# A22 × T4 of each two pairs of the MLP by seven half-size inner products, in a kernel of eight cores

## The chip, the cores and the metric

The kernel runs on the eight cores of one Trainium2 chip (two dies of four cores). Each core takes 1024 tokens and all weights; the cores exchange nothing. The metric is the device time of the slowest core in microseconds (us), over several executions.

Some executions fall into a slower state in which one or both dies run at a lower granted TensorE clock (in the profile of before die 1 had 0.967 and its cores took 1120.7 us, die 0 had 0.993 and 1091.8 us, medians of the cores). Every run is marked *fast* or *slow* for that, and only fast runs are compared here. A ratio is the mean time of one kernel's fast runs over the mean of the other's fast runs of the same rounds on the same chip. That is not quite the ratio of the medians that are quoted beside it.

## The reference, cut to what matters

The function is a decoder block: a token mixer (gating heads and pooling heads), an output projection, then a squared-ReLU MLP.

```python
D_MODEL, D_FF = 2048, 8192          # x is (2, 4096, 2048): 1024 tokens for each of eight cores
def reference(x, ...):
    ...                              # mixer and output projection, about the first 310 us
    # rmsnorm(x, g_ffn), h @ w_up, relu squared, @ w_down, residual; then the final rmsnorm
    ...
```

The MLP is done in four blocks of 2048 hidden channels. A block has an *up* part (h2T times w_up) and a *down* part (the activations `mlp` times w_down). Each part is eight *pairs*; a pair is two tiles of 128 output channels. The eight parts run from about 310 to 1040 us of the span.

## The kernel before

On each core TensorE does the matrix products, VectorE and ScalarE the sums, copies and activations, and DMA transfers are requested from queues, here mostly from the Pool queue (109.85 of the 144.48 MB in the profile of before). The kernel has TensorE add up each product in a bank of the tile `ps`, which is called a PSUM bank here. A program is written as a list of operations; a scheduler on the host, which is part of the kernel, fixes each engine's order before the launch. TensorE keeps the order in which the program writes its products. VectorE and ScalarE get an order from estimated times, the Pool queue keeps the order of the program. On the chip each engine then goes through its list in one order: all eight cores show the same sequence on VectorE (1254 instructions), ScalarE (959) and Pool (273), though their waits differ.

**A pair.** Contraction 2048 and 1024 tokens are split in halves. With A11, A12 (first tile), A21, A22 (second tile) and B11 … B22 the four blocks are made by seven products instead of eight (Strassen–Winograd). Each product is a group of eight matmuls with 512 columns. The letters below are the kernel's own:

| letter | product | letter | product |
|---|---|---|---|
| n | A11 × B11 of the *next* pair | 5 | S1 × T1 |
| 2 | A12 × B21 | 4 | A22 × T4 |
| 6 | S2 × T2 | 3 | S4 × B22 |
| 7 | S3 × T3 | | |

S1 … S4 are sums of weight blocks that VectorE makes anew for each pair. T1 … T4 are sums of activation blocks, made once for each part. n, 6, 7 and 4 add up in one PSUM bank; after n, 6 and 7 ScalarE copies the partial sum out, and the next of them may not start before that copy.

**Two pairs.** For 26 couples of pairs (an even and an odd one: 15 couples in up parts, 11 in down parts) product 2 is not made by two groups of 8 × 512. A12 of both pairs times B21 is again split in halves and made by seven products, each four matmuls of 256 columns: `q w y r` and two of `e` in the even pair, one more `e` in the odd pair.

```python
NORMAL, LAST, FIRST = "6275n43", "625s7n4", "5627n43"
NORMAL_A, NORMAL_B, LAST_B, FIRST_A = "q65w7enyr43", "657en43", "6e5s7n4", "56qe7wnyr43"

def q_sums(i):                                  # left sums of two pairs, on VectorE
    a, b = A(i, 0, 1), A(i + 1, 0, 1)           # A12 of pair i and of pair i+1
    ...
    qs[1] = ... Sq[:, 0] = b[:, 0::2, :] + b[:, 1::2, :]
    qs[2] = dve_sub(Sq[:, 1], Sq[:, 0], a[:, 0::2, :], ...)
    qs[4] = dve_sub(Sq[:, 2], a[:, 1::2, :], Sq[:, 1], ...)

def inner(c, i, R, st, b21):                    # q, w and y add up in one bank, with a copy after each
    if c == "q":
        ... pe(mms4(b, 0, A(i, 0, 1)[:, 0::2, :], I.b11, True), ...)
        q_op["s", 0] = P.add("act", ... sq[:, 0, :] <- ps[:, b, 0:HQ] ...)
    elif c == "w":
        ... pe(mms4(b, 0, Sq[:, 1], I.t2, False), ...)          # needs the copy of q
        q_op["s", 1] = P.add("act", ... sq[:, 1, :] <- ps ...)
    elif c == "y":
        ... pe(mms4(b, 0, A3(i), I.t3, False), ...)             # needs the copy of w
    ...
```

Note that the sums for `w` in the even pair i read a tile of pair i+1.

**Weight tiles.** Each pair has two tiles of 128 × 2048. They arrive in a ring of six slots, so the tiles of pair i+3 take the slots of pair i. Their requests are issued from the Pool queue when the next pair begins. In the down parts that queue also carries the accumulating stores of finished results.

```python
def load_tiles(upto=NTILE):                     # asks for tiles as long as the next slot's user is done
    while nxt[0] <= min(upto, NTILE - 1):
        ...
        elif u is not None and done[u] is None:
            break
        ...
        tile_ld[n] = P.dma("pool", ... TL(n) <- wt_d[n - NSTART] ...)

# in pair(): both slots count as done after the pair's last product
if c in "43s":
    tile_done[n0] = tile_done[n1] = st[4 if c == "4" else 3]
# in the loops over pairs: load_tiles() is called first, then pair(...)
# in StageEnd (down parts): the store, in the same Pool queue
stg_last[s] = xo_last[m, h] = P.dma("pool", ... xo_d[m] <- stg, accum_op=ALU.add ...)
```

## Time and profile before

| | us |
|---|---|
| median of the first three runs | 1090.83 (1089.46 to 1154.0, of which 1154.0 is slow) |
| fast runs | 1089.46, 1089.61, 1090.83 |

This is the view of all cores: span and mean granted clock of a core, then the median of each die.

```profile
core 0: 1092.2 us, clock 0.993
...
die 0 (median of its cores): 1091.8 us, clock 0.993
die 1 (median of its cores): 1120.7 us, clock 0.967
```

Die 0 was hardly disturbed, so core 0 is read. First the page of core 0: busy us of each engine, its share of the span, and the number of instructions; then the chain of waits, the work that ended last followed back to its releasers, as shares of the span.

```profile
PE 1070.8 (98%) x5952; PEld 548.9 (50%) x5952; DVE 684.2 (63%) x1254; ACT 473.3 (43%) x959; POOL 170.9 (16%) x273
...
PE 93%; DMA 3%; DVE 2%; POOL 1%; issue 1%; ACT 0%; DVEq 0%; ACTq 0%; POOLq 0%
```

TensorE (PE) is the bound: 98% busy and 93% of the chain. The 3% of DMA in the chain is the start of the kernel, not the MLP's tiles.

Next the timeline of TensorE on core 0 (start, duration, engine, line, operation, destination and sources, size, count), cut to the borders of two pairs in an up part. Rows of four 256-wide matmuls and of sixteen 512-wide ones let the durations be taken from start to start.

```profile
504.88 0.60 PE L537 MATMUL ps<-h2T,ring 128*128 128x256 bf16 x4
505.32 3.62 PE L537 MATMUL ps<-T,Sw 128*128 128x512 f16 x16
508.77 0.60 PE L537 MATMUL ps<-TH,Sq 128*128 128x256 f16 x4
...
517.86 3.62 PE L537 MATMUL ps<-T,Sw 128*128 128x512 f16 x16
...
528.66 0.60 PE L537 MATMUL ps<-h2T,ring 128*128 128x256 bf16 x4
```

The two pairs take 528.66 − 504.88 = 23.78 us: 12.98 for the even pair and 10.80 for the odd one. Sixteen 512-wide matmuls take 3.45 us, four 256-wide ones 0.44 us. No row carries a wait. Busy time alone would not prove that: the record of four small matmuls is 0.60 us long and the next row starts 0.44 us after it. So a record can reach 0.16 us into the next one, and a gap of less than 0.16 us does not show in the busy share here.

Last, a down part: the timeline of core 0 with all engines, cut to the store and the tile requests in the Pool queue, the first left sum that reads the tile on VectorE (DVE), and `w` on TensorE, which needs two such sums.

```profile
874.51 3.62 PE L537 MATMUL ps<-Q,Sw 128*128 128x512 f16 x16
...
876.13 0.88 POOL L1495 DMA_DIRECT2D xo<-stg  x1 [1.89 <-DVE stg L955]
...
876.70 1.44 POOL L610 DMA_DIRECT2D ring<-wt  x2
...
887.40 0.43 DVE L989 TENSOR_TENSOR Sq<-ring 128x512 f16<-128x512 bf16 x1 [0.54 <-DMA ring<-wt]
...
889.20 0.60 PE L537 MATMUL ps<-TH,Sq 128*128 128x256 f16 x4
```

The odd pair begins at 874.51.

### The profile page before, as it was taken

Reading aid. Unit: us, or ns where it says so; the run is one execution under the profiler, and the core shown is the slowest. Engines: PE = TensorE matmul, PEld = TensorE weight load, DVE = VectorE, ACT = ScalarE, POOL = GpSimd, SP = SyncE. Lnnn points to the kernel's source line nnn. Section 1 sums busy time; section 2 is a strip of 40 time slices with the busy share of each in tenths; the row PEclk is TensorE's granted clock in tenths of the full one; section 3 lists DMA queues with packets and bytes.
Section 4 is the critical chain, followed back from the end, with each engine's and each line's share of the span. In section 5 each row is a group of like instructions: output and inputs, shape, how many; then the busy total and the mean of one; then the engine's idle time right before and its main releaser. Section 6 shows DMA issues by size and latency. Waiting matters only on the chain.

```text
span 1122.8 us, 17577 instructions; the slowest of 8 cores (1091.3 to 1122.8 us)
## 1 busy us (share of the span) xinstructions
PE 1094.4 (97%) x5871; PEld 556.7 (50%) x5952; DVE 685.2 (61%) x1254; ACT 476.6 (42%) x959; POOL 170.4 (15%) x273
## 2 busy tenths in 40 slices
PE   5899999999999999999999999999999999999997
PEld 1354444444444444554454555544455544455577
DVE  1559547866687665555556555555665555556657
ACT  2421166545455552113555211355522135555574
POOL 4210024300000002221000222100022210001000
PEclk9999999999999999999999999999999999999999
DMA  9999504678768857999454799945579996469408
GB/s 213 266 169 166 94 1 80 139 197 173 139 136 161 184 98 98 133 130 139 79 92 77 101 132 133 140 75 90 80 98 134 138 167 102 80 131 202 76 6 297
DMA packets 51052, 144.48 MB, mean 129 GB/s; under 512 B 6482, under 2 KB 13650, under 8 KB 50580
## 3 DMA queue, kind: packets, MB, share of 16 engines
q0 software_dynamic: 33936, 109.85, 63.5%
q1 hardware_dynamic: 17028, 33.50, 9.5%
q8 instruction: 49, 0.80, 0.3%
q14 instruction: 39, 0.32, 0.1%
HBM read 204.14 MB, written 28.32 MB: 207 GB/s over the span
## 4 chain that ended last, share of the span: by engine, by line
PE 93%; DMA 2%; issue 2%; DVE 2%; POOL 1%; ACT 0%; DVEq 0%; ACTq 0%; POOLq 0%
PE ps L537 93%; DMA ring<-wt 2%; DVE xr_all L1615 1%; POOL ring L580 0%; DVE xh L1615 0%; POOL xst L571 0%; DVE xh L1363 0%; DVE xr_all L1363 0%; ACT sqB L1385 0%; ACT xr_all L1353 0%; DVEq L1650 0%; DVE xr_all L1392 0%; DVE xr_all L1382 0%; DVE xB L1615 0%; ACT sqr L1367 0%
## 5 line engine op out<-in xcount | busy, mean ns | idle before, releaser
L610 POOL DMA_DIRECT2D ring<-wt x158 | 92.9, 639 | 525.5 <-PE ps L537 519.4
L975 ACT ACTIVATE UC<-ps 128x512 f32<-128x512 f32 (+1 forms) x144 | 83.8, 582 | 206.5 <-PE ps L537 189.9
L537 PE MATMUL ps<-hT,ring 128*128 128x512 bf16 x501 | 118.6, 391 | 16.5 <-DMA ring<-w 14.5
L955 DVE TENSOR_TENSOR xr_all<-xr_all,ps 128x512 f32<-128x512 f32 (+1 forms) x102 | 67.2, 660 | 106.8 <-PE ps L537 106.7
L537 PE MATMUL ps<-Q,Sw 128*128 128x512 f16 x512 | 117.8, 380 | 0.0
L537 PE MATMUL ps<-T,Sw 128*128 128x512 f16 x512 | 117.6, 382 | 0.0
L537 PE MATMUL ps<-mlp,ring 128*128 128x192 bf16 (+4 forms) x755 | 100.4, 282 | 1.1
L537 PEld LDWEIGHTS ps<-hT,ring 128*128 128x128 bf16 x512 | 50.4, 100 | 80.5 <-issue 26.4
L537 PE MATMUL ps<-h2T,ring 128*128 128x512 bf16 (+1 forms) x361 | 85.5, 377 | 2.6
L955 DVE TENSOR_TENSOR rtmp<-UC,ps 128x512 f32<-128x512 f32 x64 | 43.9, 685 | 71.9 <-PE ps L537 56.9
L1432 ACT ACTIVATE rtmp<-rtmp 128x512 f32<-128x512 f32 x94 | 58.8, 629 | 67.2 <-DVE rtmp L955 67.2
L1435 ACT ACTIVATE mlp<-rtmp 128x512 bf16<-128x512 f32 x128 | 77.4, 625 | 5.8
L537 PE MATMUL ps<-h2T_t,wring 128*128 128x512 f16 (+1 forms) x316 | 79.7, 398 | 0.0
L537 PEld LDWEIGHTS ps<-Q,Sw 128*128 128x128 f16 x512 | 50.2, 98 | 58.7 <-issue 1.7
L537 PEld LDWEIGHTS ps<-T,Sw 128*128 128x128 f16 x512 | 50.3, 98 | 57.0 <-issue 2.9
L537 PEld LDWEIGHTS ps<-mlp,ring 128*128 128x128 bf16 x776 | 60.9, 99 | 33.8 <-issue 4.0
L1495 POOL DMA_DIRECT2D xo<-stg x48 | 42.4, 884 | 223.2 <-DVE stg L955 208.6
L972 ACT ACTIVATE ps<-ps 128x512 f32<-128x512 f32 (+1 forms) x72 | 41.0, 570 | 62.7 <-PE ps L537 61.6
L537 PE MATMUL ps<-T,ring 128*128 128x512 f16 x256 | 63.9, 395 | 0.0
L537 PEld LDWEIGHTS ps<-h2T,ring 128*128 128x128 bf16 x392 | 41.4, 106 | 41.6 <-issue 30.0
L537 PE MATMUL ps<-h2T,Sw 128*128 128x512 bf16 x252 | 60.8, 385 | 0.2
L537 PE MATMUL ps<-Q,ring 128*128 128x512 f16 x256 | 60.8, 381 | 0.0
(182 smaller groups left out, 1613.5 us busy)
## 6 DMA issues: line engine op xcount, KB each, us to landing
ring<-wt POOLq DMA_DIRECT2D x158, 512.0 KB, 9.0
xo<-stg POOLq DMA_DIRECT2D x48, 256.0 KB, 5.5
xr_all<-xr SPq DMA_DIRECT2D x10, 512.0 KB, 12.3
out<-xr_all SPq DMA_DIRECT2D x11, 384.0 KB, 3.7
xst<-xs POOLq DMA_DIRECT2D x8, 512.0 KB, 23.1
xo<-xr_all SPq DMA_DIRECT2D x8, 512.0 KB, 5.7
xr_all<-xo SPq DMA_DIRECT2D x8, 512.0 KB, 8.8
xst<-xs POOLq DMA_DIRECT2D x3, 1024.0 KB, 22.1
```

Source lines behind the costliest of these rows:

```text
L537: op = P.add("pe", lambda e, o=o, l=l, r=r, st=st, sp=sp: e.matmul(o, l, r, start=st, stop=sp, skip_group_check=True))
L610: tile_ld[n] = P.dma("pool", lambda e, n=n: e.dma_start(out=TL(n), in_=wt_d[n - NSTART].rearrange("p (k c) -> p k c", k=KC)), "t%d" % s, deps)
L955: return P.add("dve", lambda e: e.tensor_tensor(out=out, in0=x, in1=y, op=ALU.add), deps)
L972: st["cp", 0] = P.add("act", lambda e: e.activation(out=ps[:, b, 0:w], in_=ps[:, st["a"], 0:w], func=AF.Copy), [st[1], bank_last[b]])
L975: st["cp", u + 1] = P.add("act", lambda e: e.activation(out=UC[:, u, 0:w], in_=ps[:, st["a"], 0:w], func=AF.Copy), [st[which], uc_rd[u]])
L1432: a1 = P.add("act", lambda e: e.activation(out=t, in_=src, func=AF.Relu, scale=CA), [ready, free])
L1435: rt_rd[s] = done[h] = P.add("act", lambda e: e.activation(out=mlp[:, f, h * H:(h + 1) * H], in_=t, func=AF.Square), [a1] + deps)
L1495: stg_last[s] = xo_last[m, h] = P.dma("pool", lambda e: e.dma_start(out=xo_d[m][:, h * H:(h + 1) * H], in_=t, accum_op=ALU.add), "sg%d" % ...
L1615: o = P.add("dve", lambda e: e.tensor_tensor(out=y, in0=x, in1=r.to_broadcast(list(x.shape)), op=ALU.mult), r3[g])
```

## The change

The intent: do for product 4 (A22 × T4) what is done for product 2 already. Two groups of 8 × 512 per couple are replaced by seven products of 4 × 256, written with capital letters Q W Y R E. Their left sums, copies and right sums get buffers of their own, most of them in memory that only the last weight tiles used before; two right sums of the down parts and two of the left sums lie elsewhere, as the diff shows. The code for the small letters becomes a class that serves both.

```diff
+    TH4 = sb("TH4", [128, 3, 4, HQ], F16, LOW)
+    TA44 = sb("TA44", [128, 4, HQ], F16, LOW + 6144)
+    sq4 = sb("sq4", [128, 4, HQ], F32, LOW + 8192)
+    Sq4 = sb("Sq4", [128, 2, 4, 128], F16, LOW + 12288)
     ringL = sb("ringL", [128, 2, KC, 128], BF16, LOW)
...
+    TAx = sb("TAx", [128, 2, 4, HQ], F16, C0 + 4096)
...
-    def q_sums(i):
-    ...
+    class Quad:
+        ...
+        def s_sums(self, i):
+            a, b, S = self.A(i, 0), self.A(i + 1, 0), self.s_mem
+            ao, bo = self.A(i, 1), self.A(i + 1, 1)
+            if self.col == 0:                    # small letters, as before
+                ...
+            else:                                # capitals; two of the sums lie in tiles that are read out
+                self.S = {1: S[:, 0], 4: S[:, 1], 3: WR(self.tile(i + 1), 8), 2: WR(self.tile(i), 8)}
+                add(self.S[1], b, bo, [])
+                dve_sub(self.S[3], a, b, [])
+                dve_sub(self.S[2], self.S[1], a, [])
+                dve_sub(self.S[4], ao, self.S[2], [])
...
+    IH4 = Inner(T4, T4, TH4[:, 0], TH4[:, 1], TH4[:, 2])
+    IA4 = Inner(Q4, Q4, TAx[:, 0], TAx[:, 1], TA44[:, :, :])
+    RH.inner, RA.inner = (IH, IH4), (IA, IA4)
+    quads = (Quad(0, sq, Sq), Quad(1, sq4, Sq4))
...
-    NORMAL_A, NORMAL_B, LAST_B, FIRST_A = "q65w7enyr43", "657en43", "6e5s7n4", "56qe7wnyr43"
+    NORMAL_A, NORMAL_B, LAST_B, FIRST_A = "q65w7yQrnWeYRE3", "657enE3", "6e5s7nE", "56qe7wnQyrWEYR3"
...
         if "e" in order:
             need["11"] = "e" if i % 2 else "er"
+            need["21"] = "E" if i % 2 else "ER"
...
-                fill = fills(fill, {"6": [lambda: q_sums(i)], "5": [lambda: q_sum3(i)]})
+                fill = fills(fill, {"6": [lambda: quads[0].s_sums(i)], "5": [lambda: quads[0].s_sum3(i)], "Q": [lambda: quads[1].s_sums(i)]})
... (the evacuation adds the block of the capitals to the bank of n, 6 and 7; cut)
```

In the even pair 12 small and 5 large groups stand where 6 small and 6 large ones stood. In the odd pair one large group (4) became one small one (E).

## The prediction

> **What bounds the kernel now.** The profile of before fell in the slow state on one die only (view of all cores: cores 4 to 7 took 1118 to 1123 us at clock 0.96 to 0.97, cores 0 to 3 1091 to 1092 us at 0.99). I read core 0. TensorE is busy 98% of the span, the chain of waits is 93% matmul, and in the table of windows TensorE is busy 20.00 of every 20 us from 220 to 1060 us. In the MLP VectorE is at about 12.5 of 20 us, ScalarE at 11 (up) or 4 (down). A matmul column removed is time removed, unless its replacement brings waits.
>
> **Matmuls.** In TensorE's timeline eight 512-wide matmuls take 1.727 us (216 ns each), four 256-wide ones 0.437 us (109 ns each): small products carry almost no penalty. [...] Two pairs that already use seven inner products for A12 x B21 take 23.78 us each time: 12 x 1.727 + 7 x 0.437. The change replaces two A22 x T4 groups (3.454 us) by seven small ones (3.056 us): 0.398 us saved per two pairs. There are 26 of them (15 up, 11 down; the groups view has 26 of each copy into sq). 26 x 0.398 = 10.35 us, all on the critical path: 0.95%.
>
> **Added elsewhere.** Per two pairs three ScalarE copies of 128x256 (0.38 us each), and on VectorE four half sums (0.42 each), two 256-wide adds (0.42) and two 512-wide adds (0.69): about 3.9 us. VectorE goes from about 63% to 80% in the up parts (near 90% in the first block, which also scales x), ScalarE from 55% to 60%. Plus four sets of four small sums, 2.7 us each. None exceeds TensorE. DMA traffic and its release points hardly move; the new buffers lie where only the last weight tiles were loaded.
>
> **Where waits may come.** (1) Y follows W by only e (0.87 us), and the copy of W must fit between: today a 256-wide copy starts 0.25 us after its group and takes 0.38, so 0.73 us with an idle ScalarE. But the copy of the next pair's first product (0.58) comes just before, and in up parts a relu or square (0.63) may be in the way: 0 to 0.5 us, sometimes. (2) In odd up pairs product 3 now follows 7 by 2.6 us instead of 3.9; the copy (0.6) and VectorE add (0.69) between them now end about 2.0 us after 7, less room with a fuller VectorE. (3) W needs its left sum within 2.2 us of Q. All of it: 1 to 3 us.
>
> **Prediction.** Fast runs of before: about 1090. 1090 - 10.35 + 2 = 1081.5 us; 8 times in 10 between 1078.5 and 1087. Faster by over 2%: 0.01; within 2%: 0.96; slower by over 2%: 0.03.
>
> **What would show it.** Right: two pairs take 23.4 us in TensorE's timeline, TensorE stays 20.00 of 20 us, 312 more matmuls, VectorE about 90 us busier in total, ScalarE about 30. Wrong: gaps on TensorE before Y (released by the copy into sq4), before the 3 of odd up pairs (released by a VectorE add into rtmp), or before W; largest in the up parts.
>
> **What would make it wrong.** ScalarE's fixed order puts a relu or square before the copy of W in most up pairs (5 to 8 us more); VectorE over 90% in the first block brings the left sums late; a lower granted clock, or the slow state in most runs.

10.35 us is 26 × 0.398, from the 1.727 and 0.437 us of the trace, and the 2 us is the estimate of the waits. 1090 − 10.35 + 2 comes to 1081.65, given as 1081.5.

## The result, and the profile after

| | before | after |
|---|---|---|
| runs | 4, one of them slow | 4, all fast |
| median, us | 1090.22 | 1085.85 |
| fast runs, us | 1089.46 to 1090.83 | 1084.78 to 1086.9 |

The ratio of the fast runs is 0.9962 (95% interval 0.9943 to 0.9982). By the means, 1089.97 and 1085.85, the change gains 4.1 us. The prediction said 8.5 us (1090 to 1081.5), so a little under half came. The class, within 2%, is as predicted, and 1085.85 lies inside the range.

The view of all cores after the change:

```profile
core 0: 1082.3 us, clock 0.996
core 1: 1079.0 us, clock 0.997
core 2: 1083.9 us, clock 0.996
```

The cores now differ by 5 us at the same clock, and the slowest sets the time. The page of the slowest (core 2), with the same two lines as before:

```profile
PE 1051.1 (97%) x6183; PEld 575.8 (53%) x6264; DVE 774.3 (71%) x1478; ACT 500.6 (46%) x1037; POOL 170.3 (16%) x273
...
PE 84%; DMA 7%; DVE 3%; issue 2%; ACT 1%; POOL 1%; DVEq 0%; ACTq 0%; POOLq 0%
PE ps L542 84%; DMA ring<-wt 4%; DMA ring<-w 3%; DVE xr_all L1641 1%; DVE xh L1641 0%; POOL ring L585 0%; POOL xst L576 0%; ACT sq L1058 0%; DVE xr_all L960 0%; DVE wring L900 0%; POOL xo L1519 0%; DVE stg L960 0%; DVE zE L712 0%; DVE Sw L948 0%; DVE xh L1387 0%
```

The weight loads (PEld) went from 5952 to 6264, the 312 predicted (this core's trace lacks 81 matmul records). TensorE's part of the chain fell from 93% to 84%. What came in its place is chiefly the DMA of weight tiles, 4%, with the sums that read them and ScalarE's copies into `sq`.

The matmuls do what was promised. TensorE's timeline of core 0 at the same place, without waits:

```profile
499.85 0.60 PE L542 MATMUL ps<-h2T,ring 128*128 128x256 bf16 x4
...
513.73 3.62 PE L542 MATMUL ps<-T,Sw 128*128 128x512 f16 x16
...
523.23 0.60 PE L542 MATMUL ps<-h2T,ring 128*128 128x256 bf16 x4
```

23.38 us for two pairs, 0.40 less. But see how it is divided: the even pair is longer, 13.88 instead of 12.98, and the odd pair shorter, 9.50 instead of 10.80.

Two kinds of gap have appeared. The first lies before Y in up parts (core 0, TensorE and ScalarE):

```profile
556.13 0.63 ACT L1459 ACTIVATE mlp<-rtmp 128x512 bf16<-128x512 f32 x1
...
556.45 0.60 PE L542 MATMUL ps<-h2T,ring 128*128 128x256 bf16 x4
...
556.67 0.58 ACT L977 ACTIVATE ps<-ps 128x512 f32<-128x512 f32 x1
...
556.88 0.60 PE L542 MATMUL ps<-h2T,Sq 128*128 128x256 bf16 x4
...
557.18 0.36 ACT L1058 ACTIVATE sq<-ps 128x256 f32<-128x256 f32 x1
...
557.69 0.49 PE L542 MATMUL ps<-T,wring 128*128 128x256 f16 x3 [0.21 <-ACT sq L1058]
```

The last row is Y. It waits for the copy of W into `sq`, which stands in ScalarE's queue behind a square into `mlp` and the copy of the next pair's first product. From start to start the gap is 557.69 − 556.88 − 0.44 = 0.37 us; the bracket shows 0.21 because the record before is too long by 0.16. ScalarE takes its three instructions one after the other: each starts about when the record of the one before it ends (at 556.67 for an end at 556.76, at 557.18 for one at 557.25).

The second kind lies in the down parts (core 0, all engines, same rows as shown of before):

```profile
867.25 3.62 PE L542 MATMUL ps<-Q,Sw 128*128 128x512 f16 x16
...
868.86 0.88 POOL L1519 DMA_DIRECT2D xo<-stg  x1 [2.57 <-DVE stg L960]
...
869.43 1.44 POOL L615 DMA_DIRECT2D ring<-wt  x2
...
880.10 0.43 DVE L960 TENSOR_TENSOR Sq<-ring 128x512 f16<-128x512 bf16 x1 [1.78 <-DMA ring<-wt]
...
880.63 0.43 DVE L900 TENSOR_TENSOR Sq<-Sq,ring 128x512 f16<-128x512 f16 x1
...
881.20 0.60 PE L542 MATMUL ps<-TH,Sq 128*128 128x256 f16 x4 [0.39 <-DVE Sq L900]
```

The requests come 2.18 us after the odd pair begins, as before (2.19). But the odd pair is 1.3 us shorter, so `w` would start at 880.64, only 11.2 us after the request instead of 12.5. The tile has not got faster: VectorE waits 1.78 us for it, the left sums end late, and TensorE loses 0.56 us.

The same late tile can reach TensorE by a longer way. On core 5, in the first block, VectorE's queue stands 2.05 us for a tile; the adds behind it are late, ScalarE takes their relu and squares late, and its copy of the partial sum comes late for product 7 and the copy of W for Y. Core 1 of the same trace has no such wait at this place, no gap before 7, and only 0.31 us before this Y; core 5 has 0.90 and 1.29 us.

```profile
358.22 0.42 DVE L960 TENSOR_TENSOR Sq<-ring 128x512 f16<-128x512 bf16 x1 [2.05 <-DMA ring<-wt]
...
361.71 2.32 PE L542 MATMUL ps<-h2T_t,wring 128*128 128x512 f16 x12 [0.73 <-ACT UC L980]
...
369.07 0.60 PE L542 MATMUL ps<-T,wring 128*128 128x256 f16 x4 [1.12 <-ACT sq L1058]
```

Waits of the whole MLP can be counted in the view of waits, restricted to 330 to 1040 us (who waits, for whom: us in total, times, longest). First core 0 of before, then core 5 of after:

```profile
DVE Sw L943 <- DMA ring<-wt: 5.0, 4, 1.5
...
DVE Sq L989 <- DMA ring<-wt: 2.5, 3, 1.2
```

```profile
DVE Sw L948 <- DMA ring<-wt: 12.8, 11, 2.0
...
DVE Sq L960 <- DMA ring<-wt: 9.8, 12, 3.0
PE ps L542 <- ACT sq L1058: 1.7, 4, 1.1
...
PE ps L542 <- DVE Sq L900: 1.7, 1, 1.7
```

On these cores VectorE waited 7 times for tiles (4 and 3) and now waits 23 times (core 0 of after: 19 times). TensorE had no wait for another engine in this view of before and now waits for ScalarE and VectorE.

The size of all this on TensorE: from the traces I took the distance from each matmul's start to the next, less the time of its columns at the granted clock, and added up what exceeds 40 ns between 330 and 1040 us. The time of the columns is an estimate from the trace of before: 1.727 us for eight 512-wide and 0.437 us for four 256-wide matmuls lie on a line of about 0.417 ns a column plus 2.6 ns. It is divided by the granted clock: at 0.81, from 326 to 340 us on core 0 of before, a 512-wide matmul took 263 ns from start to start instead of 216. Only cores whose trace has all matmul records count. Before: 0.0 to 0.3 us. After: 3.1 us (core 1) to 7.2 us (core 6). The slowest core, core 2, is not among them; with its missing matmul records filled in, my estimate for it is 7.9 us. By product, the gaps of after stand before Y (2.3 to 3.6 us a core), W (0.6 to 2.0), `w` (0.0 to 1.8) and 7 (0.0 to 0.9). Core 1 has none before `w` and 7, and its Y and W gaps are 0.3 to 0.4 us each: its 3.1 us are what the new products cost without a late tile reaching TensorE.

### The profile page after: what moved, and what is told of

It reads as the page before. It is cut to its first block, busy times and chain, and to the rows that moved or that the text cites. A ratio compares the mean times of both kernels' runs of the same rounds, so it can differ in the third digit from the quotient of the medians.

```text
span 1083.9 us, 18827 instructions; the slowest of 8 cores (1079.0 to 1083.9 us)
## 1 busy us (share of the span) xinstructions
PE 1051.1 (97%) x6183; PEld 575.8 (53%) x6264; DVE 774.3 (71%) x1478; ACT 500.6 (46%) x1037; POOL 170.3 (16%) x273
## 3 DMA queue, kind: packets, MB, share of 16 engines
q0 software_dynamic: 33936, 109.85, 65.1%
## 4 chain that ended last, share of the span: by engine, by line
PE 84%; DMA 7%; DVE 3%; issue 2%; ACT 1%; POOL 1%; DVEq 0%; ACTq 0%; POOLq 0%
PE ps L542 84%; DMA ring<-wt 4%; DMA ring<-w 3%; DVE xr_all L1641 1%; DVE xh L1641 0%; POOL ring L585 0%; POOL xst L576 0%; ACT sq L1058 0%; DVE xr_all L960 0%; DVE wring L900 0%; POOL xo L1519 0%; DVE stg L960 0%; DVE zE L712 0%; DVE Sw L948 0%; DVE xh L1387 0%
## 5 line engine op out<-in xcount | busy, mean ns | idle before, releaser
L1058 ACT ACTIVATE sq<-ps 128x256 f32<-128x256 f32 x156 | 59.5, 381 | 87.7 <-PE ps L542 87.7
L1456 ACT ACTIVATE rtmp<-rtmp 128x512 f32<-128x512 f32 x124 | 76.7, 627 | 49.2 <-DVE rtmp L960 49.0
L542 PE MATMUL ps<-mlp,ring 128*128 128x192 bf16 (+4 forms) x755 | 98.2, 279 | 1.1
L542 PE MATMUL ps<-h2T,ring 128*128 128x512 bf16 (+1 forms) x361 | 75.6, 344 | 1.6
L542 PE MATMUL ps<-h2T_t,wring 128*128 128x512 f16 (+1 forms) x316 | 67.0, 359 | 1.2 <-ACT UC L980 1.2
L900 DVE TENSOR_TENSOR wring<-ring 128x1024 f16<-128x1024 bf16 (+1 forms) x116 | 65.8, 568 | 1.7
L960 DVE TENSOR_TENSOR rtmp<-sq,ps 128x512 f32<-128x512 f32 x60 | 41.3, 688 | 27.0 <-PE ps L542 18.8
L948 DVE TENSOR_TENSOR Sw<-ring 128x1024 f16<-128x1024 bf16 x70 | 48.2, 689 | 15.0 <-DMA ring<-wt 11.4
```

Of the source, the lines that this page charges most:

```text
L542: op = P.add("pe", lambda e, o=o, l=l, r=r, st=st, sp=sp: e.matmul(o, l, r, start=st, stop=sp, skip_group_check=True))
L900: return P.add("dve", lambda e: e.tensor_tensor(out=out, in0=in0, in1=in1, op=ALU.subtract), deps)
L948: s_ops[i, 1] = P.add("dve", lambda e: e.tensor_tensor(out=S[:, 0], in0=A(i, 1, 0), in1=A(i, 1, 1), op=ALU.add), ld)
L960: return P.add("dve", lambda e: e.tensor_tensor(out=out, in0=x, in1=y, op=ALU.add), deps)
L1058: return P.add("act", lambda e: e.activation(out=Q.sq[:, j, :], in_=ps[:, b, 0:HQ], func=AF.Copy))
L1456: a1 = P.add("act", lambda e: e.activation(out=t, in_=src, func=AF.Relu, scale=CA), [ready, free])
```

## The experiments

Theories:

- **A, the copy of W.** Y follows W too closely, and ScalarE's order puts other work before the copy. This is what the prediction named.
- **B, the late tile.** The shorter odd pair brings `w` closer to the request of the tile that its left sums read. VectorE waits at that sum, and TensorE with it (1.78 and 0.56 us in the rows above).
- **C, the rival: clock, head or tail.** The matmuls' gain is real, but a lower granted clock, or the parts before and after the MLP, give part of it back.

Seventeen runs were made, of twelve different kernels, in five groups, each group on one chip. All kernels but a3_plain_store compute the right result.

### First group: the change again, two orders, and stores without accumulation

**a0_after** is the changed kernel again.

> The changed kernel again, unaltered, beside the kernel before on one chip. Theory A (waits inside the new products): ratio 0.995 to 0.9975, and per core 5 to 7 us of gaps on TensorE between 330 and 1040 us, about 3.3 us of them before Y in up parts (the copy of W into sq ends late), 1 to 1.5 us before W in down parts (VectorE's left sum ends late), the rest before w or 7. Rival C (no waits: the missing 4 us is a different granted clock or the head and tail): gaps under 2 us, and a clock below that of the kernel before in fast runs, or a first matmul or tail later by 2 us or more.

Measured: median 1145.73 us because four of its six runs were slow; the two fast ones took 1087.82 and 1087.61. Before, on this chip, 1091.99. Ratio of the fast runs 0.9960 [0.9943, 0.9978]. Gaps on TensorE 4.0 to 7.2 us. The result repeats, and so do the gaps.

**a1_n_first** moves n before r, so that the copy of n is out of the way when W ends:

```diff
-    NORMAL_A = "q65w7yQrnWeYRE3"
+    NORMAL_A = "q65w7yQnrWeYRE3"
```

> One letter moved: in even pairs the next pair's first product (n) goes before r instead of after it, so that ScalarE's copy of n starts 0.44 us earlier and is out of the way of the copy of W. Same matmuls. Theory A: the 0.3 to 0.4 us gaps before Y in up parts shrink or go (3.3 us to under 1.5), gaps before W stay; 1.5 to 3 us faster than the changed kernel, ratio to before about 0.994. If the gaps before Y come from anything else (banks, DMA), they stay and the time is the same.

Measured: median 1123.87, fast runs 1089.32 to 1090.66, ratio 0.9979 [0.9965, 0.9994]. The gaps before Y shrank to 0.7 to 2.1 us a core (core 0 of the result's trace had 2.8), but the sums of all gaps are 1.6 to 7.3 us, and the largest single place is now `w`, with up to 2.7 us on a core. If A were the whole of it this kernel would have been faster than a0_after, and it was not.

**a2_rwey** puts R before W and E between W and Y: Y then follows W by three small groups and the copy has 1.3 us. The adds that need R are made where their other operand exists.

```diff
-    NORMAL_A, FIRST_A = "q65w7yQrnWeYRE3", "56qe7wnQyrWEYR3"
+    NORMAL_A, FIRST_A = "q65w7yQrnRWeEY3", "56qe7wnQyrRWEY3"
...
-            need["21"] = "E" if i % 2 else "ER"
+            need["21"] = "E" if i % 2 else "ERW"
```

> Same matmuls, other order: R before W and both halves of E between W and Y (Q r n R W e E Y 3), the adds of R after the copies that they need. W gets 0.44 us more after Q for its left sum, Y follows W by 1.75 us instead of 0.87. Theory A: gaps before Y go, gaps before W shrink by up to 0.44 us each; the gaps left are those before w and 7; 3.5 to 5 us faster than the changed kernel, about 1081 to 1082 us, ratio to before 0.991 to 0.993. Rival B (the weight tiles come late because the DMA engines are full in the down parts, so any time won at one wait is lost at the next): less than 1.5 us faster, with more gap before w or W behind VectorE sums that wait for a tile.

Measured: 1086.45, ratio 0.9949 [0.9936, 0.9962]. The gaps before Y are gone. Of those that are left (0.9 to 5.3 us a core) the largest are before `w`, 1.3 to 2.05 us on the cores with the most. Against a0_after this is 1.2 us, less than the 1.5 us named under B, and the intervals overlap. The waits of A exist (2.9 to 3.7 us a core in a0_after), but taking them away alone gained little: the gaps before `w` grew (0.0 to 1.3 us a core, then 0.1 to 3.3), and the end of the kernel became longer (see "What stays open").

**a3_plain_store** computes a wrong result (relative error 0.64): the stores of the down parts overwrite instead of accumulating. The aim is to take DMA work away from the tiles in the down parts: on core 0 the mean busy share of the DMA engines is 0.95 to 1.00 there (620 to 690 and 800 to 880 us, before and after), against 0.55 to 0.62 in the up parts of the second and third blocks (530 to 600 us in after; 530 to 610 and 715 to 795 us in before). The first edit keeps the scheduler's estimates as they were, and in the traces every engine's order is that of the changed kernel.

```diff
-        op.acc = k.get("accum_op") is not None
+        op.acc = eng == "pool" and k["out"].tensor.name == "xo" if kind == "d" else False
...
-                    out=xo_d[m][:, h * H:(h + 1) * H], in_=t, accum_op=ALU.add), "sg%d" % s, [o, xo_last[m, h]])
+                    out=xo_d[m][:, h * H:(h + 1) * H], in_=t), "sg%d" % s, [o, xo_last[m, h]])
```

> Wrong result on purpose: the stores that add to the kept rows in DRAM in the down parts become plain stores, which takes DMA work away in just the parts where the DMA engines are 96 to 100% busy. Order of instructions otherwise as in the changed kernel. Rival B: the gaps before w at the start of the last up part (0.5 to 1.8 us) and before W in down parts (1 us) go, and VectorE's waits for tiles (about 15 us in all) fall by half; 1 to 3 us faster than the changed kernel. Theory A: gaps before Y (3.3 us) stay; the 0.3 us gaps before W at the start of each down part stay too, as VectorE is only late with its own work there.

Measured: 1084.5 (1084.23 to 1084.95), ratio 0.9931 [0.9918, 0.9944]. For tiles asked for between 785 and 875 us, in the last full down part, the median time from issue to landing is 7.5 to 9.7 us over cores 0, 1, 3 and 5; in a0_after on the same chip it is 10.1 to 11.8. The waits of VectorE for tiles between 330 and 1040 us, first on core 3 of a0_after, then on core 3 of a3_plain_store:

```profile
DVE Sq L960 <- DMA ring<-wt: 12.6, 13, 2.5
DVE Sw L948 <- DMA ring<-wt: 11.9, 12, 1.9
```

```profile
DVE Sq L960 <- DMA ring<-wt: 2.5, 1, 2.5
...
DVE Sw L948 <- DMA ring<-wt: 1.5, 2, 1.2
```

On the six cores with complete records in both traces 6 to 25 such waits became 1 to 6. The gaps before `w` are gone; those before Y are still there, 2.7 to 3.3 us a core, and before W the same two of 0.3 us stand on every core. This is 3.2 us of gain (means of the fast runs) with not one matmul, copy or add moved, and it is the cleanest test of B: what TensorE lost time to was the tiles' arrival. It does not say which tile.

### Second group: a chip that stayed slow

Four kernels: the kernel before, the order of a2 together with earlier tile requests (described below), earlier requests alone, and all capitals at the end of the even pair (`"q65w7yQrne3RWEY"`).

> The kernel before, for a profile in the fast state. Theory A and B (the changed kernel loses to waits of its own): no clock dips in the MLP, spans of the eight cores within 2 us of each other, gaps on TensorE between 330 and 1040 us under 1 us, VectorE waiting about 7 us for tiles. Rival C: dips or gaps of several us on every core, so that the matmuls saved are worth more or less than 10.35 us.

> The order R W e E Y of the earlier run, and besides each weight tile's slot is asked for again right after the last matmul that reads it, ahead of the stores of the same pair in the Pool queue, instead of at the start of the next pair behind them: the first tile of a pair some 4 us, the second 1 to 2 us earlier. Theories A and B together: gaps before w, W and 7 fall under 0.5 us each, all gaps under 1.5 us per core, ratio to before 0.991 to 0.9925. If the tiles are late because the DMA engines are full (bandwidth, not issue time), VectorE waits as long as before for tiles and the time stays at 0.995.

> The changed kernel with the early requests for tiles alone. Theory: gaps before Y in up parts stay (about 3 us less the large one near 370 us), gaps before w and 7 go, W keeps 0.6 us; ratio to before 0.993 to 0.994, like the run with plain stores, but with a right result. If bandwidth is the limit: as the changed kernel, 0.996.

> The order q 6 5 w 7 y Q r n e 3 R W E Y: as in R W e E Y, but e and product 3 go before R, so that the next pair's second weight tile is needed 2.6 us later; requests for tiles as in the changed kernel. If the change is hurt because it needs that tile about 6 us earlier than the kernel before: gaps before R and W from late tiles fall to under 0.3 us each, those before w (which needs the next pair's first tile, as before) stay or grow; 0.5 to 1.5 us faster than R W e E Y. If the tiles are late whenever they are needed: as R W e E Y (0.995).

Measured: every run on this chip was slow on die 1: medians 1126.17, 1127.8, 1125.34 and 1123.07. The traces of die 0 are of use, though only that of b0_before is undisturbed; in the other three its clock is 0.983 to 0.993, which the count of gaps allows for. b0_before has spans of 1086.5 to 1087.1 us there at clock 0.997 to 0.999 and gaps of 0.0 to 0.3 us, so the kernel before truly has no waits to lose, and its cores are equal. Gaps in b1_rwey_early are 0.8 us, in b2_early 1.2 to 2.0, and in b3_quad_late 5.0 to 7.2, where Y follows W by E alone, 0.87 us as in the changed kernel, and 3.7 to 4.2 us of the gaps stand before it. That agrees with A as a mechanism. In b3_quad_late, where W comes 2.6 us later, no gap before W is left on these cores, as was expected if the second tile is what W waits for.

### Third group: another chip that stayed slow

> Order R W e E Y with the early tile requests again, because the chip of the last runs stayed in the slow state (its undisturbed die showed gaps of only 0.8 us per core, 0.7 of them before R at the start of two down parts). On a chip in the fast state: all gaps under 1.5 us on every core, spans of the cores 1078 to 1081 us, ratio to before 0.991 to 0.9925. If the time is still 0.995, the waits were not the cause, however small the gaps.

> The changed kernel with early tile requests alone, again for the fast state. Gaps before Y of about 1.5 us (five of 0.3 us) and before W 0.4 us stay, those before w, 7 and the large one before Y go; ratio to before 0.9925 to 0.994, between the changed kernel (0.996) and the run with both.

> Control: the kernel before with the same early tile requests. It has no gaps in the MLP (under 0.3 us on the undisturbed die), so if early requests help only by ending waits: ratio 0.999 to 1.001. If they help in another way (tail, DMA traffic): faster by more than 0.2%, and the gain of the other runs is not the waits' alone.

> As the first of these, with W before R in the first two pairs of a down part (W R E Y there), where R waits 0.35 us twice for a bank that ScalarE's copy of y has to free. If W's left sum is in time now: 0.7 us less gap, the same ratio within noise (0.991 to 0.9925). If VectorE is late with it: gaps before W of 0.1 to 0.3 us take the place of those before R.

Measured: 1180.56, 1178.46, 1172.4 and 1180.82 us with both dies at a clock of about 0.90 to 0.94; before took 1172.53. c3_before_early was the control for B (earlier requests in the kernel before): 0.9991 [0.9937, 1.0044], but at a clock of 0.93, so it is inconclusive. That on this chip the changed kernels were slower than before is seen in slow runs only, and I do not explain it.

### Fourth group: earlier tile requests, with and without the new order

In a couple, a tile need not be held to the pair's end. The first one is read out after e and y, the second after 7, Q, W and E. The edit marks each done there and asks for the next tile in the middle of the pair, before the pair's later stores enter the Pool queue:

```diff
             done.add(c)
+            if "E" in order:
+                for n, last in ((n0, "ey"), (n1, "7QWE")):
+                    if tile_done[n] is None and set(last) & set(order) <= done:
+                        tile_done[n] = P.all[-1]
+                        load_tiles()
```

d2_early is the changed kernel with this edit; d1_rwey_early has this edit and the order of a2_rwey. They are the kernels of b2_early and b1_rwey_early, on a chip that ran fast. The edit does more than it says: the scheduler reckons with the earlier tiles and orders VectorE and ScalarE anew. Against the changed kernel 308 of VectorE's 1478 places and 19 of ScalarE's 1037 hold another instruction (core 1's traces); TensorE's order is the same.

> Order R W e E Y with early tile requests, third try for a chip in the fast state. If the two waits (Y behind ScalarE's order, VectorE's sums behind late tiles) are what the change lost: no core with more than 1.5 us of gaps, spans of 1078 to 1082 us on all cores, ratio to before 0.9905 to 0.9925. If the shortfall is something else: 0.995 or more with gaps gone.

> Early tile requests alone. The tiles' part of the loss goes and the order's part stays (five gaps of 0.3 us before Y, two before W): ratio to before 0.9925 to 0.994.

Measured, all on one chip with before at 1090.33 (1089.29 to 1091.32): d2_early 1082.19, ratio 0.9925 [0.9913, 0.9938]; d1_rwey_early 1081.42 (1080.98 to 1082.44), ratio 0.9919 [0.9905, 0.9932]. Gaps on TensorE: 1.9 to 3.1 us in d2_early, of which 1.4 to 2.4 stand before Y; 0.8 us in d1_rwey_early. With the tiles in time A's wait is what is left, and the order of a2 takes most of it: 0.8 us of time by the medians, less than the intervals can separate, but plain in the traces, where 1.1 to 2.3 us of gaps go.

### Fifth group: which tile, and a last order

The requests are split: e1_first_tile keeps only `(n0, "ey")` of the loop above, e2_second_tile only `(n1, "7QWE")`. e3_first_wre is d1_rwey_early with `"56qe7wnQyrWREY3"` for the first couple of a down part. It is the kernel of c4_first_wre.

> The changed kernel with the early request for each pair's first weight tile alone. Shortened in the changed kernel: first tile, request to w 12.5 us to 11.2 us in down parts; second tile, needed at W some 5 us after w instead of about 10.8 us after it. If the first tile's window is what hurts: gaps before w (0.5 to 1.8 us) go and most of the gain is there (ratio 0.993 to 0.994); if the second's: gaps before W by late tiles (0.9 us), before 7 and the large one before Y near 370 us stay, ratio 0.995.

> The early request for each pair's second tile alone, 1.7 us before the end of the pair; as the Pool queue is in order, the next pair's first tile is then asked for before it, at the same point. So, if issue order matters, this helps the first tile as well, by less: gaps before w shrink but may stay at 0.2 to 0.5 us on the slowest core; ratio 0.9935 to 0.995.

> Order R W e E Y, early requests for both tiles, and W before R in the first two pairs of a down part: the two gaps of 0.35 us before R become gaps of at most 0.15 us before W; ratio 0.991 to 0.992, the best of all, 0 to 0.6 us under the version with R first.

| kernel | median, us | ratio to before [95%] | gaps on TensorE, us a core |
|---|---|---|---|
| before | 1089.93 | | 0.0 to 0.3 (trace of b0_before) |
| e2_second_tile | 1086.12 | 0.9961 [0.9947, 0.9975] | 3.3 to 6.0 |
| e1_first_tile | 1082.72 | 0.9933 [0.9920, 0.9946] | 2.2 to 3.75 |
| e3_first_wre | 1081.13 | 0.9917 [0.9903, 0.9931] | 0.83 |

e2_second_tile turned out to be no experiment on the second tile. Requests are made in order, and the first tile's slot is not free before the pair ends, so the early request of the second one never fires. Laid side by side, the instructions of its five queues are those of the changed kernel. It is therefore a third measurement of the changed kernel, on this chip, and it shows the loss again: 0.9961.

e1_first_tile against it moves one request in each pair of a couple, and with it, as in d2_early, the order on VectorE and ScalarE. It gains 3.4 us by the medians, and the two intervals just do not overlap. Not all of that is the tile's: four gaps before Y between 530 and 750 us (1.3 us together on each core, and there in a3_plain_store too) became two of 0.24 us at other places, and the two before W went from 0.3 to 0.2 us each. So about 1.0 us a core is the new order's. The gaps before `w` (0.0 to 2.2 us a core in e2) are gone, as in a3_plain_store. The timeline of core 1 of e1_first_tile, at the place shown of the other two kernels:

```profile
862.20 0.55 POOL L615 DMA_DIRECT2D ring<-wt  x1 [7.68 <-PE ps L542]
...
863.47 0.88 POOL L1524 DMA_DIRECT2D xo<-stg  x1 [0.72 <-DVE sq L960]
...
866.92 0.88 POOL L1524 DMA_DIRECT2D xo<-stg  x1 [2.57 <-DVE Sw L900]
...
867.49 0.88 POOL L615 DMA_DIRECT2D ring<-wt  x1
...
871.70 0.42 DVE L960 TENSOR_TENSOR Sq<-ring 128x512 f16<-128x512 bf16 x1
...
878.71 0.60 PE L542 MATMUL ps<-TH,Sq 128*128 128x256 f16 x4
```

The first tile is asked for at 862.20, before both stores and 16.5 us before `w`. VectorE reads it at 871.70 without a wait. Only the second tile still comes behind the stores. The waits of e1_first_tile on core 1, over the same stretch as before, and after them those of e3_first_wre on core 1:

```profile
DVE Sq L960 <- DMA ring<-wt: 7.0, 9, 2.0
...
PE ps L542 <- ACT sq L1058: 1.3, 2, 1.1
...
PE ps L542 <- ACT UC L980: 0.7, 1, 0.7
```

```profile
DVE Sq L960 <- DMA ring<-wt: 2.7, 5, 0.8
...
PE ps L542 <- DVE wring L900: 0.4, 1, 0.4
```

In e1 no wait of TensorE for a sum into `Sq` is left; what VectorE still waits for is the second tile, and TensorE's three waits in this view are for ScalarE. In e3 both tiles come early, and TensorE has two gaps of 0.36 us before W, on every core, of which this view shows one. I had hoped that its order would take these away, and it did not.

e3_first_wre is the fastest of all: 8.8 us under before by the medians, and 5.0 under the change (e2_second_tile on the same chip). It and d1_rwey_early are versions that beat both kernels; between those two there is no difference that these runs can tell.

## Why the prediction was wrong

Point by point:

- **What bounds the kernel: right.** TensorE is the bound, and before it lost 0.0 to 0.3 us in the MLP.
- **The matmuls: right.** Two pairs take 23.38 us (predicted 23.4), there are 312 more matmuls, and small products cost no more than the prediction said: from start to start a 512-wide matmul takes 216 ns and a 256-wide one 109, on core 0 of before and of after alike. The gain of 10.35 us is nearly all to be had: once the waits were taken away the kernel took 1081.1 to 1081.4 us, the time that was predicted. From the first product of the first couple to the last one of the 25th, core 2 of b0_before takes 618.4 us and e3_first_wre 609.2 on every core with complete records: 25 x 0.398 us less, but for its 0.73 us of gaps.
- **The work added elsewhere: right.** VectorE is busy 774.3 us instead of 685.2 on the slowest cores' pages, 89 more (predicted 90), ScalarE 500.6 instead of 476.6, 24 more (predicted 30). Neither is the bound.
- **"All of it: 1 to 3 us": this is the step that failed.** The sum was 1090 − 10.35 + 2, and the term of 2 us measured about 6: 10.35 predicted from matmuls less 4.1 to 4.3 gained (4.3 is 1090 × 0.0039, from e2_second_tile's ratio). The gaps on TensorE say the same: up to 7.2 us on the worst core with complete records, against 0.0 to 0.3 before, and the slowest core sets the time. About half of it is what the prediction had counted: core 1, where no late tile reached TensorE, has 3.1 us. The term that was missing is the wait for tiles, some 3 us: 3.2 went with a3_plain_store.
- **Why it failed: "DMA traffic and its release points hardly move".** As worded this is true and misses the matter. The Pool queue's traffic is 109.85 MB in both profiles, and the requests stand 2.2 us after the odd pair's start in both. What moved is the *use*: the change took 1.3 us out of the odd pair and put 0.9 into the even one, and the stretch from a tile's request to its first use lies mostly in the odd pair. It shrank from 12.5 to 11.2 us in the down parts. In the rows shown the first tile could be read 10.7 us after its request, before (876.70 to 887.40) and after (869.43 to 880.10), and the two left sums need another 1.0 us: 0.8 us to spare before, 0.5 us too late after. What is more, TensorE now needs the second tile's sums at W, 5.2 us after `w` (six groups by their durations), where it needed them at product 6 of the odd pair, 9.1 us after `w` (889.20 to 898.29 in the timeline of before; the expectation of e1_first_tile said 10.8). The prediction had three places where waits may come, and all three were copies and adds; none was a DMA.
- **Y after W: right.** It was named with its releaser, and gaps of 0.3 to 0.4 us are there as predicted (seven on core 0, of 0.31 to 0.84 us, 2.8 us in all). Six of these seven are of 0.3 to 0.4 us, stand on every core (one is 0.56 us on core 3), and stay when the tiles come in time (a3_plain_store). The seventh, near 369 us, is larger, up to 1.3 us, on cores where VectorE had waited for a tile before. By d2 to d1 another order of the products is worth about 0.8 us.
- **Product 3 of odd up pairs: wrong.** In the changed kernel's traces no gap above 0.1 us stands there, on the cores whose records are complete.
- **W: the place right, the cause in part.** Two gaps of 0.3 us, at the start of the second and third down part, stay in a3_plain_store with nearly all waits for tiles gone: there VectorE is late with its own work, as predicted. The rest, up to 1.4 us a core, mostly in down parts, is gone in a3_plain_store: there the left sum was late for the second tile.
- **"TensorE stays 20.00 of 20 us": wrong.** In core 0's table of windows it is at 19.26 at the worst, from 620 to 640 us. That fits a kernel that is not quite bound by TensorE any more.
- **Rival C: fallen.** Undisturbed cores of before (b0_before, die 0) ran at clocks of 0.997 to 0.999 and those of after at 0.996 to 0.999, TensorE's gaps from 1040 us on are 1.2 to 1.7 us in before and in nearly all versions (2.7 on one core of d1_rwey_early), and versions without gaps in the MLP have the gain without a better clock, head or tail.

What each part is worth: the late tiles together 3.2 us (a0 to a3, no order changed). On the chip of the last two groups, the first tile's earlier request with the order that the scheduler made of it 3.4 us (e2 to e1); of this some 1.0 us is the order's by the gaps. The second tile then brings 0.5 us (e1 to d2, where only four of VectorE's places differ) and the order of a2 0.8 us (d2 to d1), both by medians and both less than the intervals can separate.

What stays open: of the 10.35 us the best version shows about 9.0 (1090 × 0.0083). Its 0.83 us of gaps is one part of the rest. The other is at the end: from the start of TensorE's last matmul the kernels with the order of a2 take 6.8 to 8.2 us to finish (a2, d1 and e3, all cores), the other changed kernels 5.1 to 6.3 (after, a0, a1, a3, d2, e1 and e2), b0_before 5.9 to 6.1. So that order takes back some 1.5 us after the last product, which also hides part of its worth in the comparisons above; why it does was not looked into. Whether earlier requests would also help the kernel before was not measured in the fast state; its TensorE has at most 0.3 us of gaps in the MLP, so there is little to win.

## What to carry to other kernels

When a change shortens one step and lengthens its neighbour, write down for every prefetch the distance from its request to its first use, before and after, and compare it with the time that such a request takes to land in *that* stage; a request that neither moves nor grows can still become late. Where an engine keeps to a fixed order, as these did, a late operand is paid for by what stands behind it (on core 5 of after VectorE's wait of 2.05 us for a tile was followed by gaps of 0.90 and 1.29 us on TensorE), so look at what stands behind the wait, and put requests for the next data before stores that themselves wait. When one wait is taken away alone, expect another to take its place: in a1_n_first the gaps before Y shrank, those before `w` grew, and the kernel was no faster. And where a scheduler fixes the orders, compare the orders in the traces before you call an experiment clean: moving one request moved hundreds of VectorE's instructions.

## What else the traces showed

- The time of a weight tile from its request to landing depends on the part. The medians are 5.4 to 6.4 us in the up parts of the second and third blocks of before (530 to 600 and 715 to 785 us, cores 0, 1 and 3) and 11.0 to 11.2 us in the down parts (605 to 690 and 795 to 885 us), where accumulating stores share the queue, and up to 12.3 us in after (605 to 690 us, core 5). With plain stores it was 7.5 to 9.7 us in the third block's down part.
- The tile requests stood behind a store that waited 1.9 to 2.6 us for VectorE, and moving one of the two requests before the stores, with the order that the scheduler made of it, was worth 3.4 us of 1086.
- In fast runs eight cores ran these matmuls at a mean granted clock of 0.994 to 0.999 (all cores of the profiles of after, d1_rwey_early and e3_first_wre). Drops to 0.81, of about 15 us each, were seen twice on die 0 in the profile of before. The slow runs have lower means: about 0.96 on one die in most runs of the second group, about 0.90 to 0.94 on both dies in most of the third. In the slowest, cores of one die were at a mean of 0.811 to 0.829 (a0_after at 1297.01 us, a1_n_first at 1295.76, before at 1307.76 beside the fifth group).
- The record of four 256-wide matmuls is 0.16 us longer than the distance to the next start, so gaps below 0.16 us are invisible in the busy share and larger ones are shown too small by that much.
